# B and C of the SSM and the first MLP columns: weights as the stationary operand, high and low tokens as one moving operand

## The chip, the cores and the metric

The kernel runs on one core of a Trainium2 chip. The metric is the device time of one execution in microseconds (us), as the median of several runs.

## The reference

Two layers on 256 tokens of 2048 features, in float32: multi-head latent attention and an MLP, then a Mamba-2 mixer (SSM) and an MLP. Each part works on an RMS-normed input and adds to the residual. What the change touches:

```python
def ssm_mixer(h, w_in, conv_w, conv_b, ...):
    zxbcdt = h @ w_in                        # 2048 -> z 4096, x 4096, B 1024, C 1024, dt 64
    z, xbc, dt = jnp.split(zxbcdt, ...)
    xbc = jax.nn.silu(causal_depthwise_conv(xbc, conv_w, conv_b))   # width 4, along the tokens
    xs, b_in, c_in = jnp.split(xbc, ...)     # 8 groups: 512 of x, 128 of B, 128 of C each
    ...                                      # scan: C B^T with decay, times x dt; plus D x
    y = y * jax.nn.silu(z)                   # the gate, then an RMS norm for each group
    return (y * norm_g) @ w_out

def squared_relu_mlp(h, w_in, w_out):        # 2048 -> 8192 -> 2048
    u = jax.nn.relu(h @ w_in)
    return (u * u) @ w_out
```

## The kernel before

**Products.** Each float32 operand is split into a high part in a short format (`fp32r`, by a copy on ScalarE, L102 for weights and L299 for activations) and a low part (the rest, by a subtract on VectorE, L103 and L300). A product is three matmuls: high x high, low x high, high x low. Weights come in pieces of 512 KB (128 rows x 1024) through the pool `raw` (`wraw`, or `wrx` in the MLP), are split into `wh` and `wl`, and are converted three pieces ahead of their use. The activations are kept transposed (features on the partitions, `xT`, `us`, `yT`) and are the stationary operand: a matmul loads 128 features x 128 tokens and streams 512 weight columns. The result, 128 tokens x 512 columns, has to be transposed by TensorE before it can be the input of the next product: four 128x128 transposes into one bank (`transposed`, L310), then a split.

**Order.** TensorE's order is written out by hand; the other engines follow the order in which the code issues their work. `later(n, fn)` puts a step off by n ticks; `block` ticks after each key of two pieces. So what `later(0, ...)` names runs after the next key.

**Boundaries.** `finalize` adds a block to the residual, multiplies by the gain and puts the transposes off by a tick; the factor 1/rms (`rs`, from `set_rstd`) is applied later, to the results. `self.xT` lies in eight tiles of pool `xt`, high and low apart, either by feature quarter or (`by_tile`, for the MLPs) by feature half and token tile. The attention uses the same eight tiles for q, k, p and transposed p.

**MLP.** Of eight column pairs (two blocks of 512 hidden columns each) seven are computed by a scheme of seven products of half size (`M1`, `N3` to `N7`, `M2`), on combinations of quarters of the input that `combinations` builds in three steps (`one`, `two`, `three`). The first pair is computed plainly: tokens ("c", 0, j, o), o = 0 to 7, one piece each. `plan` writes the order of all pieces and `mlp_body` walks through it, with a clock (`move`) that puts transposes and steps at their times.

**SSM.** `SSM_ORDER` lists the blocks: B0, d0, C0, x0, B1, x1, C1, and so on. B and C are computed 512 columns (four groups) at a time, `bc_block`; ScalarE applies `rs`, TensorE transposes, and `conv` works with the tokens along the free axis (L1083 to L1095). `cb_group` makes the product of B and C for a group. `narrow_block` (L344) computes dt with the weights stationary and 256 tokens moving. `z_block` computes the gate; `gate` multiplies on GpSimd, takes square sums and a root, scales (L1317) and sends the transposes of the gated y a step later. The o blocks multiply these with `w_out`.

Of the kernel before, what the change touches and what calls it, by code (L numbers as in the profile page):

```python
# [42 lines left out]
C_INV, C_DTB, C_ALOG, C_CW, C_CB, C_END = 848, 880, 944, 1008, 1200, 1248  # L43
# [171 lines left out]
class Trunk:  # L215
    def __init__(self, tc, ctx, d, out):
# [6 lines left out]
        self.xtp = pool("xt", 8)  # L223
# [112 lines left out]
    def narrow_block(self, key, tiles, then, lag=1):  # L336
# [5 lines left out]
        for kt in range(16):  # L342
            for i in range(2):
                nc.tensor.matmul(acc[:, :256], w[kt // 8][:, kt % 8], tiles[kt // 4][i][:, kt % 4],  # L344
                                 start=kt == 0 and i == 0, stop=kt == 15 and i == 1)
# [13 lines left out]
    def from_tiles(self, tiles, off=0):  # L359
        def lhs(kt, t):  # L360
            h, lo = tiles[(kt + off) // 4]
# [5 lines left out]
    def boundary_begin(self, gain, by_tile=False):  # L367

        self.nx = {} if by_tile else [None] * 4
        self.by_tile = by_tile  # L370
        self.nx_ssq = self.stat(8)
        self.nx_gain = gain
# [6 lines left out]
    def finalize(self, nb, accs, wide=True):  # L379
        nc = self.nc  # L380
        g = self.gain_tile(self.nx_gain[nb])
        if not self.by_tile:
            self.nx[nb] = (self.ktile(self.xtp), self.ktile(self.xtp))
        elif nb % 2 == 0:
            for t in range(2):
                self.nx[nb // 2, t] = [self.ktile(self.xtp).rearrange("p a b -> p (a b)").rearrange("p (k n) -> p k n", n=P)
                                       for _ in range(2)]
        for t in range(2):
            if self.by_tile:
                h, lo = (v[:, 4 * (nb % 2):4 * (nb % 2) + 4] for v in self.nx[nb // 2, t])  # L390
            else:
                h, lo = (v[:, :, t * P:(t + 1) * P] for v in self.nx[nb])
# [12 lines left out]
    def set_rstd(self, ssq):  # L405
# [6 lines left out]
        self.nc.gpsimd.tensor_scalar(keep[:, 2:4], r, 0.5, None, ALU.mult)  # L412
        self.rs = [keep[:, t:t + 1] for t in range(2)]
        self.rsh = [keep[:, 2 + t:3 + t] for t in range(2)]

    def add_residual(self, nb, accs):
        for t in range(2):
            x = self.x[t][nb]
            self.nc.vector.tensor_tensor(x, accs[t], x, ALU.add)


    def start(self, seq):
# [28 lines left out]
        self.rs_pool = [self.c.tile([P, 4], F32, name=f"rs{i}") for i in range(2)]  # L451
        self.phase = 0
        self.xT = [(self.ktile(self.xtp), self.ktile(self.xtp)) for _ in range(4)]

        def split_x(j, ks):
            h, lo = self.xT[j]
# [41 lines left out]
    def combinations(self, mp, xa):  # L498
# [4 lines left out]

        def whole(i, t):
            pool = "rx" if len(f) < 3 else "ry"
            f[i, t] = self.flow.pools[pool].tile([P, 1024], F32, tag=pool, name=self.name("xf"))
            h, lo = (v.rearrange("p k n -> p (k n)").bitcast(F32) for v in xa[i, t])
            nc.vector.tensor_tensor(f[i, t], h, lo, ALU.add)
            return f[i, t]

        def put(name, src, pool):
            S[name] = [(self.ktile(self.xtp).rearrange("p a b -> p (a b)") if pool is None else
                        pool.tile([P, 1024], F32R, name=self.name("s" + name))).rearrange("p (k n) -> p k n", n=P)
                       for _ in range(2)]
            self.split_out(*[v.rearrange("p k n -> p (k n)") for v in S[name]], src)
# [5 lines left out]
        def one():  # L521
# [3 lines left out]
            put("N5", a22, mp)  # L525
            f["s1"] = a22

        def two():
            put("N7", less(f[0, 1], f[0, 1], f[0, 0]), mp)
            put("N6", less(f[0, 0], f[0, 0], f["s1"]), mp)  # L530
# [3 lines left out]
        def three():  # L534
            put("N3", f[1, 0], None)
# [3 lines left out]
    def mlp_body(self, mp, layer, gain):  # L539
# [12 lines left out]
        def relu(src, t):  # L552
            r = self.scratch()
            nc.scalar.activation(r, src, AF.Relu, scale=rs[t])
            return r

        def lhs_x(kt, t):
            return [v[:, kt % 8] for v in xa[kt // 8, t]]
# [5 lines left out]
        S["M1"], S["N4"], S["M2"] = xa[0, 0], xa[1, 1], xa[1, 0]  # L564
# [69 lines left out]
        for tok in tokens:  # L634
            key = (tok[0], layer) + tok[1:]
            if tok[0] == "s":
# [8 lines left out]
                products([bank[name]], key, lambda k, t: [x[:, k] for x in S[name]], d,  # L645
# [4 lines left out]
            elif tok[0] == "c":  # L650
                _, p, j, o = tok
                if o == 0:
                    out["c"] = pair_of_banks(self.yp if j else self.acc)
                products(out["c"], key, lhs_x, o, o == 0, o == 7)
                if o == 7:
                    for t in range(2):
                        turn(relu(out["c"][t], t), p, j, t, TR[4])
                    if j:
                        when(3, steps[2])
                if o % 2:  # L660
                    self.tick()
                move(2.72)
            else:
# [4 lines left out]
                if o == 3:  # L668
                    self.add_residual(nb, out.pop(nb))
# [134 lines left out]
    def mla_body(self, mp, gain):  # L804
# [90 lines left out]
        def s1(u, name):  # L895
# [3 lines left out]
            dst = self.ktile(self.xtp, F32)  # L899
# [22 lines left out]
        def s2(u):  # L922
            qT, kT = U[u]["qT"], U[u]["kT"]
            p = self.ktile(self.xtp, F32).rearrange("p a b -> p (a b)")
# [25 lines left out]
        def s3(u):  # L950
            p = U[u]["p"]
            pT = self.ktile(self.xtp, F32).rearrange("p a b -> p (a b)")
# [58 lines left out]
        self.boundary_begin(gain, True)  # L1011
# [26 lines left out]
    def ssm_body(self, sp, dp, gain):  # L1038
# [11 lines left out]
        fm = {}  # L1050
        xg = [None] * GROUPS
        early = [True]
# [23 lines left out]
        def conv(ev, ct, dst, lag):  # L1076

            def half(j):
                b = self.bank(early[0])
                for k in range(2):  # L1080
                    for t in range(2):
                        o = k * 256 + t * P
                        nc.tensor.transpose(b[:, o:o + P], ev[t][:, (2 * j + k) * P:(2 * j + k + 1) * P], self.ident)  # L1083
                a = self.scratch()
                for k in range(2):
                    c = ct + 2 * j + k
                    wc = lambda i: cst[:, C_CW + 4 * c + i:C_CW + 4 * c + i + 1]
                    s, o = b[:, k * 256:(k + 1) * 256], a[:, k * 256:(k + 1) * 256]
                    nc.scalar.activation(o, s, AF.Identity, bias=cst[:, C_CB + c:C_CB + c + 1], scale=wc(3))
                    for i in (2, 1, 0):  # L1090
                        m = 3 - i
                        nc.vector.scalar_tensor_tensor(o[:, m:256], s[:, 0:256 - m], wc(i), o[:, m:256], ALU.mult, ALU.add)
                th = self.scratch()
                nc.scalar.activation(th, a, AF.Tanh, scale=0.5)
                nc.vector.scalar_tensor_tensor(dst(j), th, 1.0, a, ALU.add, ALU.mult)  # L1095
            self.later(lag, lambda: half(0))
            self.later(lag + 1, lambda: half(1))

        def evac(accs):
            ev = []  # L1100
            for t in range(2):
                e = self.scratch()
                nc.scalar.activation(e, accs[t], AF.Copy, scale=rs[t])
                ev.append(e)
            return ev

        def bc_block(name, i):
            accs = self.block([("si", name, i, q) for q in range(4)], xT)
            t = self.ktile(self.k4, F32)
            fm[name, i] = t  # L1110
            conv(evac(accs), (32 if name == "B" else 40) + 4 * i,
                 lambda j: t[:, 2 * j:2 * j + 2].rearrange("p a b -> p (a b)"), 0)
# [50 lines left out]
        def cb_group(g):  # L1163
            B, C = fm["B", g // 4][:, g % 4], fm["C", g // 4][:, g % 4]
            b = self.bank(early[0])
            nc.tensor.matmul(b[:, 0:256], B[:, 0:P], C, start=True, stop=True)
            nc.tensor.matmul(b[:, 256:384], B[:, P:256], C[:, P:256], start=True, stop=True)
            t = sp.tile([P, 384], F32, tag="cb", name=f"cb{g}", bufs=5)
# [10 lines left out]
        def x_block(g):  # L1179
# [59 lines left out]
            if g >= 4:  # L1239
                self.later(0, lambda: cb_group(g))  # L1240
# [52 lines left out]
        def z_block(g):  # L1293
# [11 lines left out]
            def gate():  # L1305
# [10 lines left out]
                for t in range(2):  # L1316
                    nc.vector.scalar_tensor_tensor(ws[t], xg[g][t], r[:, t:t + 1], ng, ALU.mult, ALU.mult)  # L1317
                    self.later(0, lambda t=t: self.transposes(ws[t], yT[g][0], yT[g][1], t, False))
                self.later(0, lambda: gated.add(g))
# [6 lines left out]

        for step in SSM_ORDER:
            kind, i = step[0], int(step[1])
            if step == "C1":
                early[0] = False  # L1330
            if kind in "BC":
                bc_block(kind, i)
                if step == "C0":
                    for g in range(4):
                        self.later(2 + g % 2 + 4 * (g // 2), lambda g=g: cb_group(g))
                    self.pump = pump
# [9 lines left out]
            else:  # L1346
                self.boundary_begin(gain, True)
# [12 lines left out]
SSM_ORDER = ["B0", "d0", "C0", "x0", "B1", "x1", "C1", "x2", "z0", "x3", "z1", "x4", "z2", "o0", "x5", "z3", "x6", "z4", "o1",  # L1360
             "x7", "z5", "z6", "o2a", "z7", "o2b", "o3"]
# [7 lines left out]
PAUSE = 2.7  # L1369

# [57 lines left out]
def sequence(d):  # L1428
# [23 lines left out]
    def mlp(i):  # L1452
        mi, mo = d[f"mi{i}"], d[f"mo{i}"]
        unit = [seven(i, p, mi) for p in range(8)]
        for tok in plan():
            if tok[0] == "s":
                seq.append(lambda flow, t=tok: [unit[t[1]](flow, *t[2:])])
            else:
                kind, p, j, o = tok
                src = mi[o // 2, 2 * p + j] if kind == "c" else mo[2 * p + o // 2, j]  # L1460
# [6 lines left out]
    col = lambda name, i: {"z": 0, "x": 8, "B": 16, "C": 18}[name] + i  # L1467
    si = lambda name, i: [add(("si", name, i, q), d["si"][q, col(name, i)]) for q in range(4)]
    so = lambda k, nb: add(("so", k, nb), d["so"][k, nb])
    for step in SSM_ORDER:  # L1470
        kind, i = step[0], int(step[1])
        if kind in "xzBC":
            si(kind, i)
        elif kind == "d":
# [30 lines left out]

def narrow(w):
# [57 lines left out]
```

## Time and profile before

| | us |
|---|---|
| median of 3 runs | 2300.64 (2300.29 to 2302.55) |
| the profiled execution | 2299.97 |
| its span, first to last instruction | 2298.2 |
| TensorE busy in it (PE) | 2285.3 |
| VectorE busy (DVE) | 1908.4 |
| ScalarE busy (ACT) | 1392.4 |
| GpSimd busy (POOL) | 213.2 |

The granted TensorE clock was 1.000 over the span. In the rows L12 is line 12 of the kernel, `out<-in` are tile names, `xN` is a count of instructions. A timeline row gives start, duration, engine and, in brackets, idle time before it and what ended it. The rows of the grouped lines give busy time, mean ns of one, and idle time before them. PEld is TensorE's loading of the stationary operand, which has a record of its own. Matmuls overlap their neighbours in the records, so the distance between starts says more than a duration.

### The profile page before, as it was taken

The page shows a single profiled execution, that of the slowest core. Times are in us where ns is not written, and L with a number is a line of the kernel's source. Part 1 is how long each engine was busy: PE and PEld are TensorE (multiplying, and loading weights), DVE is VectorE, ACT ScalarE, POOL GpSimd, SP SyncE. Part 2 cuts the span into 40 slices and gives each one's busy share as a digit, 9 for nine tenths or more (in the row PEclk, how much of TensorE's full clock was granted, in tenths as well). Part 3 has the DMA queues.
Part 4 walks back from the last instruction along what each step waited for, and adds up shares of the span by engine and source line. Part 5 has one row for each costly group of instructions (what it writes and reads, how often), then busy time and mean ns, then how long its engine had stood idle before and what let it go on. Part 6 is the DMA issues. An engine that isn't in the chain of part 4 may idle for free.

```text
span 2298.2 us, 30453 instructions
## 1 busy us (share of the span) xinstructions
PE 2285.3 (99%) x10929; PEld 1897.3 (83%) x10929; DVE 1908.4 (83%) x2318; ACT 1392.4 (61%) x1947; POOL 213.2 (9%) x229
## 2 busy tenths in 40 slices
PE   9999999999999999999999999999999999999999
PEld 7898888888888888888888878878888888888887
DVE  7786697999899897687889678667989989989885
ACT  7775476566566656564656545544666666666663
POOL 1430000000000000000122112110000000000000
PEclk9999999999999999999999999999999999999999
DMA  8435687887887878667877777766688788888874
GB/s 316 149 126 158 198 233 244 262 239 251 264 244 245 267 209 274 203 211 245 282 258 255 248 272 239 229 187 204 206 256 236 247 265 248 243 270 239 254 224 163
DMA packets 161912, 538.07 MB, mean 234 GB/s; under 512 B 17680, under 2 KB 26832, under 8 KB 160736
## 3 DMA queue, kind: packets, MB, share of 16 engines
q1 hardware_dynamic: 151264, 502.44, 66.1%
q0 software_dynamic: 8096, 29.41, 7.9%
q10 hardware_dynamic: 2400, 4.27, 0.5%
q8 instruction: 86, 1.41, 0.2%
q14 instruction: 66, 0.54, 0.1%
HBM read 529.65 MB, written 6.41 MB: 233 GB/s over the span
## 4 chain that ended last, share of the span: by engine, by line
PE 94%; DVE 3%; DMA 1%; issue 1%; POOL 1%; ACT 1%; SPq 0%; DVEq 0%; ACTq 0%; POOLq 0%
PE acc L325 12%; PE acc L326 12%; PE acc L329 12%; PE yp L595 9%; PE yp L596 9%; PE yp L594 9%; PE st L595 7%; PE st L596 7%; PE st L594 7%; PE sm L310 2%; DVE wl L103 1%; DMA wraw<-mi 1%; PE acc L594 1%; PE acc L596 1%; PE acc L595 1%
## 5 line engine op out<-in xcount | busy, mean ns | idle before, releaser
L102 ACT ACTIVATE wh<-wraw 128x1024 fp32r<-128x1024 f32 (+1 forms) x818 | 857.9, 1053 | 606.4 <-PE acc L326 290.8
L103 DVE TENSOR_TENSOR wl<-wraw,wh 128x1024 fp32r<-128x1024 f32 (+1 forms) x818 | 984.5, 1218 | 239.0 <-ACT wh L102 228.0
L594 PE MATMUL yp<-wh,k 128*128 128x512 f32 x896 | 349.8, 390 | 0.0
L595 PE MATMUL yp<-wl,k 128*128 128x512 f32 x896 | 348.9, 389 | 0.5 <-DVE wl L103 0.5
L596 PE MATMUL yp<-wh,k 128*128 128x512 f32 x896 | 348.9, 389 | 0.0
L325 PE MATMUL acc<-wh,xt 128*128 128x512 f32 x704 | 279.3, 397 | 0.8 <-ACT wh L102 0.8
L326 PE MATMUL acc<-wh,xt 128*128 128x512 f32 x704 | 274.4, 390 | 0.0
L102 ACT ACTIVATE wh<-wrx 128x1024 fp32r<-128x1024 f32 x168 | 177.9, 1059 | 136.9 <-PE yp L596 105.0
L103 DVE TENSOR_TENSOR wl<-wrx,wh 128x1024 fp32r<-128x1024 f32 x168 | 203.8, 1219 | 37.3 <-ACT wh L102 37.2
L595 PEld LDWEIGHTS yp<-wl,k 128*128 128x128 f32 x896 | 168.3, 188 | 36.0 <-DVE wl L103 1.4
L596 PEld LDWEIGHTS yp<-wh,k 128*128 128x128 f32 x896 | 168.2, 188 | 34.9
L594 PEld LDWEIGHTS yp<-wh,k 128*128 128x128 f32 x896 | 168.2, 188 | 34.7
L325 PE MATMUL acc<-wh,k 128*128 128x512 f32 x496 | 196.2, 396 | 0.0
L326 PE MATMUL acc<-wh,k 128*128 128x512 f32 x496 | 193.2, 389 | 0.0
L329 PE MATMUL acc<-wl,xt 128*128 128x512 f32 x704 | 188.3, 389 | 0.0
L594 PE MATMUL st<-wh,xt 128*128 128x512 f32 x448 | 176.8, 395 | 0.0
L595 PE MATMUL st<-wl,xt 128*128 128x512 f32 x448 | 174.8, 390 | 0.0
L596 PE MATMUL st<-wh,xt 128*128 128x512 f32 x448 | 174.8, 390 | 0.0
L325 PEld LDWEIGHTS acc<-wh,xt 128*128 128x128 f32 x704 | 132.2, 188 | 30.8 <-ACT wh L102 3.2
L326 PEld LDWEIGHTS acc<-wh,xt 128*128 128x128 f32 x704 | 132.3, 188 | 27.6 <-issue 1.2
L329 PEld LDWEIGHTS acc<-wl,xt 128*128 128x128 f32 x704 | 132.1, 188 | 27.7
L199 POOL DMA_DIRECT2D wrx<-mi x56 | 49.1, 876 | 1140.8 <-DVE wl L103 1034.9
(307 smaller groups left out, 3449.5 us busy)
## 6 DMA issues: line engine op xcount, KB each, us to landing
wraw<-mi SPq DMA_DIRECT2D x256, 512.0 KB, 5.2
wraw<-mo SPq DMA_DIRECT2D x256, 512.0 KB, 5.3
wraw<-si SPq DMA_DIRECT2D x160, 512.0 KB, 5.0
wraw<-so SPq DMA_DIRECT2D x64, 512.0 KB, 4.8
wrx<-mi SPq DMA_DIRECT2D x56, 512.0 KB, 5.1
wrx<-mi POOLq DMA_DIRECT2D x56, 512.0 KB, 8.0
wraw<-wo SPq DMA_DIRECT2D x32, 512.0 KB, 3.9
taps<-xD SPq DMA_DIRECT2D x16, 768.0 KB, 8.4
```

Of the source, the lines that this page charges most:

```text
L102: self.last = nc.scalar.activation(h[:, v], raw[:, v], AF.Copy)
L103: self.last_lo = nc.vector.tensor_tensor(lo[:, v], raw[:, v], h[:, v].bitcast(F32), ALU.subtract)
L199: nc.gpsimd.dma_start(st["b11"].tile, quarter(d, 1, 0), accum_op=ALU.add)
L310: self.nc.tensor.transpose(b[:, j * P:(j + 1) * P], src[:, j * P:(j + 1) * P], self.ident)
L325: nc.tensor.matmul(accs[t][:, :n], ah, wh[:, q, :], start=first and kt + q == 0, stop=False)
L326: nc.tensor.matmul(accs[t][:, :n], al, wh[:, q, :], start=False, stop=False)
L329: nc.tensor.matmul(accs[t][:, :n], lhs(kt + q, t)[0], wl[:, q, :], start=False, stop=en and q == nk - 1)
L594: nc.tensor.matmul(b, ah, wh, start=first and q == 0, stop=False)
L595: nc.tensor.matmul(b, ah, wl, start=False, stop=False)
L596: nc.tensor.matmul(b, al, wh, start=False, stop=last and q == 1)
```

## The change

1. **Weights stationary** for B, C and the first column pair of each MLP. `column_unit` takes a weight piece of 1024 rows x 128 columns as eight stationary operands: the high weights multiply high and low tokens as one moving operand of 2 x 256 columns, the low weights the 256 high tokens. The two halves of the bank are added afterwards. The result has the columns on the partitions, so nothing is transposed. For this, high and low of `xT` lie in one tile (`pair`), by feature quarter throughout; `xt` has four such tiles, the attention shares them (q with k, p with transposed p), and N3 is written over the quarter of the input that is free by then.
2. **B, C group by group**: `SSM_ORDER` has a step b for each group (four pieces) between the x and z blocks. `rs` is applied by a product with `row`, the factors of the tokens along the free axis on all partitions, which two small matmuls make. In the MLP the factor is applied squared when the first pair's products are added to the residual.
3. **Gated y a step later**: its transposes stand two ticks behind the gate, not one.

```diff
+    def pair(self, dt=F32R):
+        return self.xtp.tile([P, 2, 4, 256], dt, tag="xt", name=self.name("xt"))
...
-    def add_residual(self, nb, accs):
+    def add_residual(self, nb, accs, scale=None):
...
+            if scale:
+                self.nc.vector.scalar_tensor_tensor(x, accs[t], scale[t], x, ALU.mult, ALU.add)
...
+    def column_unit(self, acc, unit, xw, half):
+        h, lo = (v.rearrange("p (k n) -> p k n", n=P) for v in unit)
+        nc = self.nc
+        high = lambda k: nc.tensor.matmul(acc.rearrange("p (i n) -> p i n", i=2), h[:, k], xw[2 * half + k // 4][:, :, k % 4],
+                                          start=half == 0 and k == 0, stop=half == 1 and k == 7)
+        low = lambda k: nc.tensor.matmul(acc[:, 0:256], lo[:, k], xw[2 * half + k // 4][:, 0, k % 4], start=False, stop=False)
+        for k in range(8):
+            for fn in ((low, high) if half and k == 7 else (high, low)):
+                fn(k)
...
         def three():
-            put("N3", f[1, 0], None)
+            for c in range(2):
+                src = f[1, 0][:, c * 512:(c + 1) * 512].rearrange("p (k n) -> p k n", n=P)
+                self.split_out(part(0, 1, c, 0), part(0, 1, c, 1), src)
+            S["N3"] = operand(0, 1)
...
+        def column(p, j, f, acc):
+            if f == 0:
+                us[p, j] = (self.ktile(self.k4), self.ktile(self.k4))
+            h, lo = us[p, j]
+            r = self.scratch()[:, 0:256]
+            nc.scalar.activation(r, acc[:, 256:512], AF.Copy)
+            nc.vector.tensor_tensor(r, acc[:, 0:256], r, ALU.add)
+            nc.scalar.activation(r, r, AF.Relu)
+            nc.scalar.activation(r, r, AF.Square)
+            self.split_out(h[:, f], lo[:, f], r)
...
-                if o % 2:
+                if o % 2 == 0:
                     self.tick()
-                move(2.72)
+                move(2.78)
...
+        def rs_row():
+            c = self.scratch()[:, :S]
+            for t in range(2):
+                nc.vector.tensor_scalar(c[:, t * P:(t + 1) * P], tri[:, P:256], rs[t], None, ALU.mult)
+            b = self.bank(False)
+            for t in range(2):
+                nc.tensor.matmul(b[:, t * P:(t + 1) * P], c[:, t * P:(t + 1) * P], self.ident, start=True, stop=True)
+            nc.vector.tensor_copy(row, b[:, :S])
+        self.later(1, rs_row)
+
+        def bc_columns(g):
+            accs = [self.acc_tile() for _ in range(2)]
+            for half in range(2):
+                for i in range(2):
+                    self.column_unit(accs[i], self.flow.next(("sb", i, g, half))[1], self.xT, half)
+                    if i == 0:
+                        self.tick()
+            s, a, th = (self.scratch() for _ in range(3))
+            of = lambda v: v.rearrange("p (i n) -> p i n", i=2)
+            for i in range(2):
+                nc.scalar.activation(of(s)[:, i], accs[i][:, 256:512], AF.Copy)
+                nc.vector.tensor_tensor(of(s)[:, i], accs[i][:, 0:256], of(s)[:, i], ALU.add)
+            def conv():
+                nc.vector.tensor_tensor(of(s), of(s), row.unsqueeze(1).to_broadcast([P, 2, S]), ALU.mult)
...
+            self.later(0, conv)
+            self.later(2, lambda: cb_group(g))
...
-                    self.later(0, lambda t=t: self.transposes(ws[t], yT[g][0], yT[g][1], t, False))
-                self.later(0, lambda: gated.add(g))
+                    self.later(1, lambda t=t: self.transposes(ws[t], yT[g][0], yT[g][1], t, False))
+                self.later(1, lambda: gated.add(g))
...
-SSM_ORDER = ["B0", "d0", "C0", "x0", "B1", "x1", "C1", "x2", "z0", "x3", "z1", "x4", "z2", "o0", "x5", "z3", "x6", "z4", "o1",
-             "x7", "z5", "z6", "o2a", "z7", "o2b", "o3"]
+SSM_ORDER = ["b0", "d0", "x0", "b1", "x1", "b2", "x2", "z0", "b3", "x3", "z1", "b4", "x4", "z2", "o0", "b5", "x5", "z3",
+             "b6", "x6", "z4", "o1", "b7", "x7", "z5", "z6", "o2a", "z7", "o2b", "o3"]
...
+def column_of(o):
+    return 2 * (o // 4) + o % 2, o % 4 // 2
```

More of the change, by code (lines that the diff above doesn't have):

```diff
@@ L651, in mlp_body @@
                 _, p, j, o = tok
[L652 to L659, printed above, removed]
-                if o % 2:
+                f, half = column_of(o)
+                if half == 0:
+                    pool = self.yp if j else self.acc
+                    out["c", f] = pool.tile([P, 512], F32, tag=pool.name, name=self.name("cf"))
+                self.column_unit(out["c", f], self.flow.next(key)[1], xa, half)
+                if half:
+                    column(p, j, f, out.pop(("c", f)))
+                if o == 7 and j:
+                    when(3, steps[2])
+                if o % 2 == 0:
                     self.tick()
-                move(2.72)
+                move(2.78)
             else:
@@ L668, in mlp_body @@
                 if o == 3:
-                    self.add_residual(nb, out.pop(nb))
+                    self.add_residual(nb, out.pop(nb), None if p else self.rssq)
                 move(2.72)
@@ L1099, in evac @@
[L1099 to L1112, printed above, removed]
+        row = sp.tile([P, S], F32, name="rsrow")
@@ L1325, in o_block @@
             return self.block([("so", 2 * i + q, nb) for q in range(2)], self.from_tiles(yT[2 * i:2 * i + 2]))
+        self.pump = pump
         for step in SSM_ORDER:
             kind, i = step[0], int(step[1])
[L1329 to L1336, printed above, removed]
+            if kind == "b":
+                bc_columns(i)
             elif kind == "d":
@@ L1471, in sequence @@
         kind, i = step[0], int(step[1])
-        if kind in "xzBC":
+        if kind in "xz":
             si(kind, i)
+        elif kind == "b":
+            for half in range(2):
+                for j in range(2):
+                    seq.append(part(("sb", j, i, half), d["sbc"][j, i, half]))
         elif kind == "d":
```

143 lines of the change are left out of this document (67 added, 76 removed).

## The prediction

> **What bounds the kernel now.** I read the page first: its shares of busy time and the chain that ended last.
>
> ```profile
> PE 2285.3 (99%) x10929; PEld 1897.3 (83%) x10929; DVE 1908.4 (83%) x2318; ACT 1392.4 (61%) x1947; POOL 213.2 (9%) x229
> ...
> PE 94%; DVE 3%; DMA 1%; issue 1%; POOL 1%; ACT 1%; SPq 0%; DVEq 0%; ACTq 0%; POOLq 0%
> ```
>
> The kernel is TensorE's own instruction stream: 94% of the chain and 99% busy. What the change is worth is therefore (a) what it takes out of and puts into that stream, and (b) which of the few waits of TensorE it ends or makes. VectorE at 83% is the next candidate. Since busy matmuls overlap in the records, I price a matmul by the distance from one start to the next. The timeline of TensorE and the chain in order of time give it.
>
> ```profile
> 962.82 0.39 PE L325 MATMUL acc<-wh,xt 128*128 128x512 f32 x1
> ...
> 965.54 0.39 PE L325 MATMUL acc<-wh,xt 128*128 128x512 f32 x1
> ...
> 977.53 0.60 PE L1083 MATMUL sm<-cst,s 128*128 128x128 f32 x4
> 977.89 0.48 PE L325 MATMUL acc<-wh,xt 128*128 128x512 f32 x1
> 978.20 0.39 PE L326 MATMUL acc<-wh,xt 128*128 128x512 f32 x1
> ```
> ```profile
> 973.86 3.83 PE sm L344 x32
> ...
> 2283.76 11.20 PE acc L703 x72
> ```
>
> From 962.82 to 965.54 lie the 12 matmuls of one weight piece: 2.72 us, 227 ns each for 512 columns. The 32 matmuls of `narrow_block` have 256 columns and a weight load each: 3.83 / 32 = 120 ns. The last block (24 of 512 columns, 48 of 256, by its code) confirms both: 24 x 0.227 + 48 x 0.120 = 11.2 us. A group of four transposes moves the second matmul behind it from 977.53 + 0.227 = 977.76 to 978.20, so it costs 0.44 us.
>
> **The change on TensorE.** Of old, a 128x128 block of weights costs three times 128 columns of output for each of two token tiles: 768 columns. In `column_unit` it is 512 (high weights on high and low tokens) and 256 (low weights on high tokens): 768 again. Only the number of instructions grows. B and C were 4 blocks of 16 x 6 = 384 matmuls; the first column pairs of the two MLPs are another 384, as these rows show (each has two partners of 64, on L595 and L596).
>
> ```profile
> L594 PE MATMUL acc<-wh,xt 128*128 128x512 f32 x64 | 25.2, 393 | 0.0
> L594 PE MATMUL yp<-wh,xt 128*128 128x512 f32 x64 | 25.1, 392 | 0.0
> ...
> L1083 PE MATMUL sm<-cst,s 128*128 128x128 f32 x20 | 3.0, 272 | 0.0
> ...
> L1083 PE MATMUL yp<-cst,s 128*128 128x128 f32 x12 | 1.8, 273 | 0.0
> ```
>
> So 768 matmuls become 512 of 512 columns and 512 of 256 columns: 512 x 0.120 - 256 x 0.227 = 61.4 - 58.1 = **+3.3 us**. Bounds: if the short ones cost half of a long one, 0; with 0.130 in the alternation of long and short, +8.5. I take the row, since there too every matmul follows its own load.
>
> The Trainium skill (page "TensorE: Matmul & The Clock Gate", section "Back-to-back issue gap") gives 262 and 518 cycles at 2.4 GHz for 256 and 512 columns, 109 and 216 ns, by which this term would be about +0.7 us, an estimate. The measured distances, 120 and 227 ns, are both 11 ns longer, so the trace decides.
>
> Transposes that go: all 32 of B and C (L1083, 8 groups), and in each MLP two column blocks x two token tiles = 4 groups, 8 in all. 16 x 0.44 = **-7.0 us**. `rs_row` adds two 128-column products, half a group: **+0.25 us**. The products of `cb_group` stay. The scaling by rs[t] of B and C becomes a product with `row`, that of the MLP columns goes into `add_residual` as rs squared, at one VectorE instruction either way.
>
> **The gated y.** Where does TensorE wait at all? The waits view has one long entry for it, and the timeline one example:
>
> ```profile
> PE sm L310 <- DVE s L1317: 5.5, 5, 1.6
> ```
> ```profile
> 1204.42 2.21 POOL L283 TENSOR_TENSOR st<-st,mhalf 128x2 f32<-128x2 f32 x1 [9.36 <-DVE st L282]
> ```
> ```profile
> 1209.21 1.75 DVE L1317 SCALAR_TENSOR_TENSOR s<-xtm,st,gb 128x512 f32<-128x512 f32 x1
> ```
> ```profile
> 1211.11 0.63 PE L310 MATMUL sm<-cst,s 128*128 128x128 f32 x4 [1.65 <-DVE s L1317]
> ```
>
> The transposes of the gated y stand one step (two pieces, 5.4 us) behind the gate in TensorE's order, and the gate's chain (product on GpSimd, square sums, root, two scalings on VectorE) ends up to 1.6 us after their turn. One step later they have 5.4 us more, over three times the longest wait. **-5.5 us**. What is late next? The o blocks that read y come at least four pieces (10.9 us) behind the moved transposes, except o2a, whose first two pieces (5.4 us) read the earlier group; I cost it at 0. The two scratch tiles of the gate stay occupied 5.4 us longer, and the B, C chain wants three of the same seven: that wait would be one of VectorE, ScalarE or GpSimd, and is part of the next term.
>
> **VectorE and ScalarE.** Here the change costs work, and I ask where there is room.
>
> ```profile
> 284.00:295.00 11.00, 11.00 (x50) 9.13 (x49) 11.00 (x11) 7.24 (x7) 0.00 (x0) 1.00 0.72 227
> 295.00:306.00 11.00, 11.00 (x53) 8.91 (x53) 10.97 (x11) 7.64 (x10) 0.00 (x0) 1.00 0.64 213
> 306.00:317.00 11.00, 11.00 (x51) 9.09 (x50) 10.94 (x11) 6.82 (x7) 1.08 (x1) 1.00 0.82 239
> 317.00:328.00 11.00, 11.00 (x50) 9.13 (x49) 10.19 (x10) 6.50 (x7) 0.87 (x1) 1.00 0.86 259
> ```
> ```profile
> 294.68 2.35 DVE L103 TENSOR_TENSOR wl<-wraw,wh 128x1024 fp32r<-128x1024 f32 x2
> ...
> 295.73 0.39 PE L594 MATMUL yp<-wh,xt 128*128 128x512 f32 x1
> ...
> 295.96 0.49 PE L595 MATMUL yp<-wl,xt 128*128 128x512 f32 x1
> ```
>
> The columns are span, PE, PEld, DVE and ACT busy time. In the first 45 us of an MLP VectorE is full (third number), because the combinations of `one` and `two` stand there, and the piece at 295.73 gets its low half at the very moment at which TensorE wants it. Into this stretch and the next go, for each MLP, 8 columns with an add and a subtract of 256 elements, in place of 4 subtracts of 512, and four sums cut in two.
>
> ```profile
> 977.73 0.42 DVE L347 COPY s<-sm 128x256 f32<-128x256 f32 x1 [2.42 <-PE sm L344]
> ```
> ```profile
> 274.24 1.28 DVE L396 TENSOR_TENSOR s<-x,gb 128x512 f32<-128x512 f32 x2
> ```
> ```profile
> 273.07 0.39 PE L594 MATMUL acc<-wh,xt 128*128 128x512 f32 x1
> ...
> 278.51 0.60 PE L310 MATMUL yp<-cst,s 128*128 128x128 f32 x4
> ```
>
> A 256 instruction takes 0.42 us; two of 512 take 1.28, so in a row each counts 0.60, some 0.08 less than alone, and one of 256 about 0.34. 16 x 0.34 - 4 x 0.60 + 4 x 0.07 = +3.3 us for each MLP. Against it: the tick now comes after the first piece of the c block, so that the last transposes of the boundary, at 278.51 after the two pieces that begin at 273.07, come one piece earlier, and `one`, which stands behind their halves in VectorE's order, can start 2.7 us sooner. Their input is ready at 274.24 + 1.28 = 275.5, before TensorE gets there at 273.07 + 8 x 0.347 = 275.85. Idle time of 0.9 us in the last two windows is also there. TensorE itself comes 4 x 0.44 - 16 x 0.05 = 0.9 us sooner. 3.3 - 2.7 - 0.9 + 0.9 = 0.6 us short for each MLP. On top, the subtract of a column needs three passes of ScalarE (Relu, Square, Copy) after the add; if VectorE stands still for them, that is up to 3 x 0.41 us a column:
>
> ```profile
> L1263 ACT ACTIVATE mt<-mt 128x256 f32<-128x256 f32 x64 | 26.1, 407 | 0.5
> ```
>
> Bounds for each MLP: 0 (the order fills the pause with other work and the head start carries) to 0.6 + 8 x 1.2 = 10 us. I take 1.0, near the lower end, because in the first two windows VectorE, whose order holds many such subtracts behind a ScalarE copy (every low half is one), is idle 0.03 us in 22. Both MLPs: **+2 us**.
>
> In the SSM, B and C bring 2 x 0.42 + 0.68 = 1.5 us of VectorE for each group (two adds, the product with `row`), and the convolution now falls between the x and z blocks. VectorE has room there (1075 to 1560 us, grouped lines: 75.8 us of idle time before the low halves alone):
>
> ```profile
> L103 DVE TENSOR_TENSOR wl<-wraw,wh 128x1024 fp32r<-128x1024 f32 x164 | 202.3, 1246 | 75.8 <-ACT wh L102 75.1 <-DMA cm<-cumD 0.4
> ```
>
> `cb_group` follows its B, C pieces by three ticks (16 us) for a chain of some 7 us of work. I take **+1 us** (0 to 6) for places where the new step meets the tail of x.
>
> Loads keep their size and queue (512 KB by SP). The pairs in `xt` are freed as late as the later of the old two, and the attention uses four of them in the rhythm in which it used eight halves: 0. If the write of N3 into half of a tile makes the M1 products of the other half wait, that is up to 2 us in each MLP; it belongs to the upper end.
>
> **Sum.** Profiled execution 2299.97 us (span 2298.2 and 1.8 around it): -7.0 + 3.3 + 0.25 - 5.5 + 2 + 1 = -5.95, so 2294.0. The median lies 0.67 above that execution: **2294.7 us**.
>
> **The rivals.** *No change:* VectorE and ScalarE give back most of the 9 us: each column halts VectorE for half of the three passes, 16 x 0.6 = 9.6 us, instead of the 2 taken: 2302. For it: VectorE at 11.00 of 11.00. Against it: three pieces of lead elsewhere, and pauses only in the first 45 us.
>
> *Slower:* the subtract waits in VectorE's queue for the whole ScalarE chain, with the low halves of the next pieces behind it and TensorE behind those. 20 us in both MLPs in place of 2: 2312.7. It decides as soon as the new waits pass 13.5 us (2291.7 without any, 2305.2 the bound), 0.84 us a column.
>
> *Slower, by the weights:* a load is not covered behind a matmul of 256 columns. The loads are long enough:
>
> ```profile
> L344 PEld LDWEIGHTS sm<-xt,wh x32: 188/192/192, 28.6 to 975.4; 128*128 128x128 f32 x32
> ```
>
> 256 more instructions x 0.19 us would be 49 us: 2344. Against it stand the 120 ns of that very line, less than one load. The Trainium skill (same page, "What overlaps and what doesn't") has loads overlap running matmuls only in other row groups, which speaks for this rival; the 120 ns of full-height loads disagree.
>
> That the change does not do what it says has little room: TensorE's order is written out by hand, and the transposes are no longer in it.
>
> **How the numbers follow.** About 0.2%, 4.6 us, is what a measurement of this kernel can tell from no change. Forecast 0.58 (2290 to 2296, all faster), no change 0.24 (2296 to 2305), the wait on ScalarE or its like 0.15, uncovered loads 0.03. The range starts at 2290 (no new waits, and short matmuls a little cheaper) and ends at 2304, which leaves the two slower cases out.
>
> **What would show it.** Right: 64 transposes less; low column products at starts 120 ns apart from the next, 347 for a pair; no wait of the y transposes for L1317's successor; VectorE busy some 18 us more (2 x 3.3 and 8 x 1.5). Wrong: TensorE idle for the low halves in the first 70 us of an MLP (VectorE rival), or pairs well above 350 ns (weights).

## The result and the profile after

The changed kernel takes 2307.6 us (2304.97 to 2310.83 in eight runs) against 2300.9 us of the kernel before in as many runs: a ratio of 1.0026, 95% interval 1.0016 to 1.0037. It is slower by some 6 us (6.7 by the medians) where 2294.7 was forecast: about 13 us more than forecast. The profiled execution after took 2310.83 us, the longest of the eight, so its own times stand some 3 us above the median.

First the page of the changed kernel: busy time by engine, and the shares of the chain that ended last.

```profile
PE 2290.7 (99%) x11125; PEld 1908.9 (83%) x11125; DVE 1930.3 (84%) x2379; ACT 1398.8 (61%) x1997; POOL 208.5 (9%) x233
...
PE 84%; DVE 9%; DMA 3%; issue 2%; POOL 1%; ACT 1%; SPq 0%; DVEq 0%; ACTq 0%; POOLq 0%
```

Busy shares look as before (99%, 83 to 84%). The chain doesn't: TensorE falls from 94% to 84% of it and VectorE rises from 3% to 9%. More of the end is now handed on by VectorE, and that sends the reader to the waits of TensorE, here those of the changed kernel (total, count, longest, in us).

```profile
PE sm L1199 <- DVE k L303: 5.1, 2, 2.8
PE acc L332 <- DVE wl L103: 2.6, 4, 1.3
PE st L620 <- DVE wl L103: 1.7, 2, 0.9
PE sm L1199 <- DVE bc L1142: 1.6, 1, 1.6
...
PE cf L427 <- DVE wl L103: 1.1, 1, 1.1
```

The wait of the y transposes for the gate, 5.5 us before, is gone. In its place the product of B and C in `cb_group` (L1199) waits 6.7 us, and 5.1 of them not for B and C but for L303, the low half of a transposed block.

Where in the kernel is the time? The first matmuls of the two MLPs, in the timelines of before (the first stands in the prediction, at 273.07) and after, divide it.

```profile
951.04 0.39 PE L325 MATMUL acc<-wh,xt 128*128 128x512 f32 x1
...
1618.82 0.47 PE L594 MATMUL acc<-wh,xt 128*128 128x512 f32 x1
```
```profile
272.70 0.39 PE L425 MATMUL cf<-xt,wh 128*128 128x512 f32 x1
...
952.17 0.39 PE L425 MATMUL acc<-xt,wh 128*128 128x512 f32 x1
...
1628.34 0.48 PE L425 MATMUL cf<-xt,wh 128*128 128x512 f32 x1
```

From the first MLP's first matmul to the SSM's: 677.97 us before, 679.47 after, +1.5. SSM: 667.78 and 676.17, +8.4. The second MLP to the end of the span: 679.4 and 680.7, +1.3. So nearly all lies in the SSM, for which the forecast's terms give -6.1 (8 groups of transposes -3.5, half of the short matmuls +1.65, `rs_row` +0.25, gated y -5.5, VectorE +1): 14.5 us off in this execution. The timeline after shows one of the long waits.

```profile
1178.75 1.03 PE L313 MATMUL sm<-cst,s 128*128 128x128 f32 x8
...
1181.95 2.45 DVE L1139 SCALAR_TENSOR_TENSOR s<-s,cst,s 128x255 f32<-128x255 f32 x6
...
1185.45 0.69 DVE L1142 SCALAR_TENSOR_TENSOR bc<-s,s 128x512 f32<-128x512 f32 x1
...
1187.26 1.28 DVE L303 TENSOR_TENSOR k<-sm,k 128x512 fp32r<-128x512 f32 x2
...
1188.00 1.22 PE L1199 MATMUL sm<-bc 128*128 128x256 f32 x2 [2.76 <-DVE k L303]
```

At 1178.75 the eight transposes of a gated y fill two banks called `sm`; the pool has no more. Their split (L303) stands in VectorE's order behind the convolution of B and C (L1139, L1142) and a step of x (L1251), and comes 8.5 us later. B and C themselves are ready at 1186.14; the first of the two banks is free only when the first of the two splits ends, at about 1187.9, and TensorE stands idle for 2.76 us. The granted clock falls during the other long wait (2.35 us, to 1120.61) and at the end of this one, as these rows show (span, then busy time of PE, PEld, DVE, ACT, POOL, then the granted clock, DMA share, GB/s):

```profile
1119.70:1126.40 6.70, 5.80 (x70) 5.18 (x71) 5.24 (x11) 3.37 (x11) 1.80 (x2) 0.50 0.49 143
1188.00:1191.30 3.30, 3.30 (x9) 2.73 (x10) 3.30 (x6) 0.00 (x0) 0.25 (x1) 0.50 0.48 176
```

TensorE works at a granted clock of 0.50 for 5.8 us behind the one wait and for 3.3 us behind the other: half of that, 4.6 us, is lost on top of the 6.7. The mean clock of this execution was 0.998; six of the other seven had 0.999 and one 1.000, so the median run lost less.

### The profile page after: what moved, and what is told of

Its sections match the earlier page's. It is cut to its first block, busy times and chain, and to the rows that moved or that the text cites. A ratio compares the mean times of both kernels' runs of the same rounds, so it can differ in the third digit from the quotient of the medians.

```text
span 2309.0 us, 30976 instructions
## 1 busy us (share of the span) xinstructions
PE 2290.7 (99%) x11125; PEld 1908.9 (83%) x11125; DVE 1930.3 (84%) x2379; ACT 1398.8 (61%) x1997; POOL 208.5 (9%) x233
## 4 chain that ended last, share of the span: by engine, by line
PE 84%; DVE 9%; DMA 3%; issue 2%; POOL 1%; ACT 1%; SPq 0%; DVEq 0%; ACTq 0%; POOLq 0%
PE acc L328 10%; PE acc L329 10%; PE acc L332 10%; PE yp L620 8%; PE yp L621 8%; PE yp L619 8%; PE st L620 7%; PE st L621 7%; PE st L619 7%; DVE wl L103 4%; PE sm L313 2%; PE acc L425 1%; DMA wraw<-mi 1%; DVE xtm L1243 1%; DVE wraw L183 1%
## 5 line engine op out<-in xcount | busy, mean ns | idle before, releaser
L620 PE MATMUL yp<-wl,k 128*128 128x512 f32 x896 | 349.0, 389 | 0.2 <-DVE wl L103 0.2
L328 PE MATMUL acc<-wh,xt 128*128 128x512 f32 x576 | 229.2, 398 | 0.4 <-ACT wh L102 0.4
L329 PE MATMUL acc<-wh,xt 128*128 128x512 f32 x576 | 225.2, 391 | 0.0
L620 PEld LDWEIGHTS yp<-wl,k 128*128 128x128 f32 x896 | 168.2, 188 | 35.4 <-DVE wl L103 0.9
L620 PE MATMUL st<-wl,xt 128*128 128x512 f32 x448 | 174.8, 390 | 0.0
L332 PE MATMUL acc<-wl,xt 128*128 128x512 f32 x576 | 154.3, 390 | 1.9 <-DVE wl L103 1.9
L332 PE MATMUL acc<-wl,k 128*128 128x512 f32 x496 | 132.9, 390 | 0.7 <-DVE wl L103 0.7
L620 PE MATMUL st<-wl,sN 128*128 128x512 f32 x336 | 131.1, 390 | 1.7 <-DVE wl L103 1.7
L619 PE MATMUL st<-wh,sN 128*128 128x512 f32 x336 | 132.1, 393 | 0.0
```

What stands on the lines that cost most here:

```text
L328: nc.tensor.matmul(accs[t][:, :n], ah, wh[:, q, :], start=first and kt + q == 0, stop=False)
L329: nc.tensor.matmul(accs[t][:, :n], al, wh[:, q, :], start=False, stop=False)
L332: nc.tensor.matmul(accs[t][:, :n], lhs(kt + q, t)[0], wl[:, q, :], start=False, stop=en and q == nk - 1)
L619: nc.tensor.matmul(b, ah, wh, start=first and q == 0, stop=False)
L620: nc.tensor.matmul(b, ah, wl, start=False, stop=False)
```

## The experiments

Ratios are to the kernel before in the runs of the same chip, with 95% intervals. The changed kernel stands at 1.0026. The kernel before had medians of 2299.5 to 2300.9 us in these batches, so a measured time is held against an expected one through the ratio.

Two theories at first. **A:** the loss is a meeting: the y transposes, a step later, hold both `sm` banks when `cb_group` comes to its turn. **B:** the loss lies in the new B, C step itself (its VectorE work, the price of its matmuls), and the later y still brings its 5.5 us.

**e1: the later y alone, in the kernel before.**

```diff
-  self.later(0, lambda t=t: self.transposes(ws[t], yT[g][0], yT[g][1], t, False))
-self.later(0, lambda: gated.add(g))
+  self.later(1, lambda t=t: self.transposes(ws[t], yT[g][0], yT[g][1], t, False))
+self.later(1, lambda: gated.add(g))
```

> The kernel before with part 3 alone: the transposes of the gated y two ticks behind the gate. Theory A (the loss of the whole change comes from B, C and the moved transposes meeting in TensorE's order, part 3 alone does what the prediction said): the five waits of the y transposes go, 5.5 us, nothing takes their place: 2295.4 us against 2300.9. Theory B (the scaling steps of the gate are only a symptom of a full VectorE, the wait comes back elsewhere): 2299 to 2301.

0.9985 (0.9977 to 0.9994), some 3.4 us faster. That is less than A's 5.5 us and more than the 1.9 that B left at most. The gate's waits are gone, but A's "nothing takes their place" did not hold; from its timeline:

```profile
1214.11 1.03 PE L310 MATMUL sm<-cst,s 128*128 128x128 f32 x8
...
1222.14 1.28 DVE L300 TENSOR_TENSOR k<-sm,k 128x512 fp32r<-128x512 f32 x2
...
1222.87 0.70 PE L1166 MATMUL sm<-k,k 128*128 128x256 f32 x2 [2.27 <-DVE k L300]
```

The same meeting, once, in the old kernel: L1166 is `cb_group`'s product there. It is the move of y that makes it, with or without the new B and C.

**e2: the y transposes back to their old place, in the changed kernel** (the same lines, 1 to 0).

> The changed kernel without part 3: y transposes one tick behind the gate again. Theory A: the products of B and C no longer wait for the two small banks that the y transposes hold (5.1 us of idle time and some 2 us of slower clock behind them), but the gate's own waits may return (0 to 5 us): 2301 to 2306 against 2307.6. Theory B: the banks play no part, the gate's waits return in full: 2311 to 2313.

1.0052 (1.004 to 1.0065): slower than the change by some 6 us. From its waits:

```profile
PE sm L313 <- DVE s L1348: 9.7, 10, 2.0
PE sm L1199 <- DVE bc L1142: 3.2, 3, 2.5
```

The wait for the bank is gone as A said, so the banks do play a part, against B. But the wait for the gate comes back at 9.7 us in ten places, where the kernel before had 5.5 in five, and A had allowed at most 5. A's number missed; B's number, 2311 to 2313, held, though not for B's reason. What it says of part 3: moving y pays, in the changed kernel more than in the old; its meeting with `cb_group` takes it back.

**e3: `cb_group` one tick later**, so that the banks are free by then.

```diff
-            self.later(2, lambda: cb_group(g))
+            self.later(3, lambda: cb_group(g))
```

> The changed kernel with the product of B and C one tick (two pieces, 5.4 us) later. Theory A: all three waits of that product go (6.7 us idle and some 2 to 3 us of slower clock behind them): 2298 to 2300 against 2307.6. Theory B: VectorE is behind anyway, and the wait moves to the low halves of the weights: 2305 to 2307.

0.9994 (0.9985 to 1.0003), 7.4 us less than the change, as A expected. No wait of L1199 is left, and the mean clock is 1.000. From its waits:

```profile
PE acc L332 <- DVE wl L103: 3.5, 6, 1.3
```

So the waits for the bank, the one for B and C, and the clock behind them are over half of the 13 us missed. Whether it was the bank or B, C that came too late, e3 does not tell, since a tick helps both.

**e9: the product of B and C in a bank of another pool**, at its old time. The far part is copied out at once, because it would hold one of the blocks' banks.

```diff
-            b = self.bank(False)
+            b = self.bank("acc")
...
-            def far_part():
-                with behind("last"):
-                    nc.scalar.activation(t[:, P:256], b[:, P:256], AF.Copy, scale=0.125)
-
-            self.later(0, far_part)
+            with behind("last"):
+                nc.scalar.activation(t[:, P:256], b[:, P:256], AF.Copy, scale=0.125)
```

> The changed kernel, with the product of B and C in a bank of the big pool (acc) in place of one of the two small banks, and all of it copied out in one step. Bank theory (two of the three waits are for a small bank that the y transposes hold until VectorE has split them): 2.5 and about 2 of the 2.9 us go, the third wait (1.8 us, for the convolved B and C themselves) stays: 2302 to 2304 against 2307.6. Rival (the convolution is late in all three): the waits keep their size, now named after the convolution's last step: 2307.

1.0003 (0.9994 to 1.0012), some 5.3 us less than the change, where the bank theory gave 3.6 to 5.6 and its rival next to nothing. The timeline at the place shown above:

```profile
1171.98 1.03 PE L313 MATMUL sm<-cst,s 128*128 128x128 f32 x8
...
1178.69 0.69 DVE L1142 SCALAR_TENSOR_TENSOR bc<-s,s 128x512 f32<-128x512 f32 x1
...
1179.52 0.67 PE L1199 MATMUL acc<-bc 128*128 128x256 f32 x2 [1.06 <-DVE bc L1142]
...
1180.49 1.29 DVE L303 TENSOR_TENSOR k<-sm,k 128x512 fp32r<-128x512 f32 x2
```

Now the product runs before the split that it used to wait for, and what is left of the wait is for B and C, 1.06 us here and 2.7 in two places in all, against 6.7 in three before. The mean clock is 1.000 again. The bank carries most of it; B and C are late as well, but less.

**e8: the meeting taken out of e1**: y later, and `cb_group` a tick later for the groups from 4 on, all else as before.

```diff
-                self.later(0, lambda: cb_group(g))
+                self.later(1, lambda: cb_group(g))
```

> The kernel before with the y transposes a tick later (e1_gate_only, 2296.2 us) and, for groups 4 to 7, the product of B and C a tick later too. If that product waits because the y transposes hold the two small banks until VectorE has split them (2.3 us, once, in e1_gate_only), the wait goes: 2293 to 2295. If VectorE is simply behind there, the wait moves: 2296.

**0.9971** (0.9959 to 0.9982), 2294.15 us against 2300.85: faster than both kernels, and as the bank theory expected. From its timeline, where e1 had the wait:

```profile
1214.04 1.03 PE L310 MATMUL sm<-cst,s 128*128 128x128 f32 x8
...
1222.09 1.27 DVE L300 TENSOR_TENSOR k<-sm,k 128x512 fp32r<-128x512 f32 x2
...
1226.67 0.59 PE L1166 MATMUL sm<-k,k 128*128 128x256 f32 x2
```

That is 6.7 us from three numbers in three calls of `later`: two move y (e1's edit), one moves `cb_group`.

**e6: the MLP part alone**, with the SSM wholly as before and y at its old time. The edit is long; its core:

```diff
-SSM_ORDER = ["b0", "d0", "x0", "b1", ...
+SSM_ORDER = ["B0", "d0", "C0", "x0", ...
...
-    a["sbc"] = columns(wi[:, 8192:10240]).reshape(2, 8, 2, P, 1024)
+    a["si"] = pieces(wi[:, :10240])
```

> The MLP part alone: first column pairs with the weights stationary, the SSM wholly as before (blocks of four groups, y transposes one tick behind the gate). Theory C: 2.5 to 4 us more than before, 2302 to 2304. Rival D: 0 to 2 us less than before.

1.0012 (1.0004 to 1.0021), +2.8 us (0.9 to 4.8), as C expected. By the forecast's terms this part was +0.15 (8 groups -3.5, short matmuls +1.65, VectorE +2).

**e5: e3 with the old first column pairs of the MLPs**, on the new layout of the tokens.

```diff
-                self.column_unit(out["c", f], self.flow.next(key)[1], xa, half)
-                if half:
-                    column(p, j, f, out.pop(("c", f)))
+                products(out["c"], key, lhs_x, o, o == 0, o == 7)
+                if o == 7:
+                    for t in range(2):
+                        turn(relu(out["c"][t], t), p, j, t, TR[4])
```

> The kernel with the product of B and C one tick later (e3_cb_later, 2299.2 us), and in both MLPs the first column pair computed as before (three matmuls, transposes, rs applied to the result); the SSM stays changed. Theory C (the MLP part costs: its short and long pairs are 352 and not 347 ns, and VectorE's low halves come late at two places for each MLP): 2.5 to 4 us less, 2295 to 2297. Rival D (the MLP part is worth its 3.5 us of transposes and what is left of the loss lies in the SSM): 2300 to 2302.

1.001 (1.0001 to 1.0019): some 3.7 us more than e3, far from C's 2.5 to 4 less and above D's range, which its interval still reaches. It brought waits of its own:

```profile
PE acc L616 <- DVE wl L103: 3.2, 2, 1.6
```

These stand 22 us into each MLP, where the kernel before has none, so this is not the old MLP, and the run doesn't settle between C and D.

**e4: high and low of a token pair next to each other**, so that the 512 moving elements lie in one stretch. It asks whether the moving operand's layout sets the price of a pair.

```diff
+    def near_pair(self):
+        return self.xtp.tile([P, 4, 2, 256], F32R, tag="xt", name=self.name("xt")).rearrange("p k i n -> p i k n")
```

> The changed kernel with high and low tokens of a feature row side by side (512 elements in a run) in place of two runs of 256 that lie 1024 elements apart. If the two runs are why a matmul of 512 columns takes 235 ns to the next start here and 227 elsewhere: pairs of 347 ns and 2.6 us less over 512 pairs, 2305. If the 8 ns come from the following short matmul's load: pairs stay at 352 ns, 2307.6.

1.0025 (1.0014 to 1.0035), as the change. The interval alone could hide 2.6 us, but the trace does not: from a long matmul to the next short one it is 235 ns in the median, as in the changed kernel. The layout isn't it.

**e7: e3 with eight high matmuls and then eight low ones** instead of turn about.

```diff
+        for k in range(7 if half else 8):
+            high(k)
         for k in range(8):
-            for fn in ((low, high) if half and k == 7 else (high, low)):
-                fn(k)
+            low(k)
+        if half:
+            high(7)
```

> e3_cb_later with the order inside a weight piece changed: first the eight long matmuls with the high weights, then the eight short ones with the low weights. If a pair takes 352 ns because long and short alternate: 347 ns, 2.6 us less over 512 pairs. If each costs that by itself, 352 ns stay. Besides, the low half of a piece is wanted 1.6 us later, so waits for low halves at column pieces (1.2 us in each run) go: 2295 to 2298 against 2299.2; or 2298 if the pairs stay.

0.9994 (0.9985 to 1.0003), level with e3. The waits for low halves at column pieces are gone as expected, but those of the MLPs' other products (L623, L620 in e3) grew from 1.9 to 2.6 us. The timelines of the changed kernel, at two places, and of e7 give the price of a pair:

```profile
1089.65 0.39 PE L425 MATMUL acc<-xt,wh 128*128 128x512 f32 x1
...
1091.38 0.39 PE L425 MATMUL acc<-xt,wh 128*128 128x512 f32 x1
...
1095.89 0.40 PE L425 MATMUL acc<-xt,wh 128*128 128x512 f32 x1
...
1097.66 0.40 PE L425 MATMUL acc<-xt,wh 128*128 128x512 f32 x1
```
```profile
1088.14 2.00 PE L425 MATMUL acc<-xt,wh 128*128 128x512 f32 x8
1089.98 1.12 PE L427 MATMUL acc<-xt,wl 128*128 128x256 f32 x8
1090.93 1.78 PE L425 MATMUL acc<-xt,wh 128*128 128x512 f32 x7
```

Turn about, five pairs take 1.73 us at one place and 1.77 at the other: 346 and 354 ns each. Grouped, a piece of eight pairs takes 2.79 us, 349. Taken over whole pieces, the median pair is 352 ns in the changed kernel and 348 in e7, so at 512 pairs the order is worth some 2 us by the records, no more than these runs resolve.

What e3 and e7 still wait for in the SSM are low halves of weights (L332: 3.5 and 3.6 us). The convolution of B and C stands in VectorE's order among the products of x with the filter there. e10 and e11, two ways out of e7, test whether that makes the low halves late.

**e10: the convolution two ticks later** and `cb_group` two more behind it; the two scratch tiles of the convolution are taken only then.

```diff
-            s, a, th = (self.scratch() for _ in range(3))
+            s = self.scratch()
...
             def conv():
+                a, th = self.scratch(), self.scratch()
...
-            self.later(0, conv)
-            self.later(3, lambda: cb_group(g))
+            self.later(2, conv)
+            self.later(5, lambda: cb_group(g))
```

> e7_high_first (2299.2 us) with the convolution two ticks later and the product of B and C two ticks after that, behind the tail of the x block before. If the low halves in the SSM come late (3.6 us in six waits) because convolution and tail of x meet on VectorE: 2295 to 2297. If VectorE is late there for another reason (its products of x slowed by GpSimd, which works at the same time): 2298 to 2300.

0.998 (0.9971 to 0.9989), about 3.2 us less than e7, as expected if the two meet, and the waits for low halves shrink to:

```profile
PE acc L332 <- DVE wl L103: 1.1, 3, 0.4
```

**e11: the ticks of the steps b1 to b7 a piece later.** It was meant to keep the filter's products on VectorE apart from GpSimd's gate product, beside which they run slower. The changed kernel's timeline shows both cases:

```profile
1091.10 4.07 POOL L1342 TENSOR_TENSOR xtm<-s,xtm 128x512 f32<-128x512 f32 x2 [6.21 <-DVE s L1332]
1091.54 2.47 DVE L1238 TENSOR_TENSOR taps<-taps,cw 128x1536 f32<-128x1536 f32 x1
1093.94 1.78 DVE L1239 TENSOR_TENSOR xtm<-xtm,cw 128x512 f32<-128x512 f32 x1
1095.65 1.75 DVE L1238 TENSOR_TENSOR taps<-taps,cw 128x1536 f32<-128x1536 f32 x1
1097.32 0.68 DVE L1239 TENSOR_TENSOR xtm<-xtm,cw 128x512 f32<-128x512 f32 x1
```

```diff
-                    if i == 0:
+                    if i == (g > 0):
                         self.tick()
```

> e7_high_first with the ticks of steps b1 to b7 after the second piece of a pair, not the first, so that the products of x with the filter are issued a piece (2.8 us) later against the gate's product on GpSimd. If the two slow each other (VectorE's filter products took 54.3 us in e3_cb_later and 44.3 before, the difference all in SSM steps where both run): 48 us or less, fewer waits for low halves, 2295 to 2297. If the overlap is not what makes the low halves late: 2299.

0.9997 (0.9989 to 1.0006): no gain. The filter's products (L1238 and L1239) still take 52.0 us, against 54.3 in e3 and 44.3 before, so the edit hardly did what it was for. Whether the overlap with GpSimd costs the kernel time stays open; e10 lost its waits with the overlap as it was (54.2 us).

**e12: e10 and e11 together.**

> Both of e10_conv_later and e11_tick. If the two causes add up: 2293 to 2295, level with e8_gate_cb (2294.2), which has neither B, C nor MLP columns; this is the best that the change can give with TensorE's pairs at 348 ns. If they are one cause: as the better of the two.

0.9981 (0.9972 to 0.999), 2294.66 us against 2299.51, as e10: e11's later tick adds nothing. The changed kernel, mended in its order alone, gains some 4.4 us, where 6 were forecast for it. That its time equals the forecast 2294.7 is luck, since the kernel before was faster in this batch. It comes no further than e8 (0.9971), which has none of its new products.

## Why the prediction was wrong

**The step that failed** is in "The gated y", the answer to "What is late next?", and its echo in the VectorE term. The prediction went through who reads the moved y transposes (the o blocks, at least 10.9 us behind) and who shares their scratch tiles, and costed the rest at nothing. It did not ask who else uses the two banks that the transposes write, and how long they hold them. For `cb_group` it priced the chain of B and C (three ticks for 7 us of work: +1 us, 0 to 6), and not the bank that its own product needs. And 7 us of work is not the time until it is done: from the last matmul on a group's columns to its convolved B and C lie 9.5 to 19 us in the trace after, 18 to 19 in the three groups that wait. The bank comes back only when VectorE has done the split, and VectorE's order has the convolution before it. In the profiled execution that was two waits of 5.1 us in all, one of 1.6 for B and C, and 4.6 us of clock behind the long ones; e1, e3, e8 and e9 show it from four sides, and e3 puts it at 7.4 us in the median.

**The second miss** is the same VectorE term: the low halves of x weights beside the convolution (2.6 us here, 3.5 in e3). "VectorE has room there" was read from idle time over 485 us. It is not there in the places where the convolution meets the filter. e10 puts it at 3.2 us. Together 10.6 of some 13 us.

**Right, with sizes.** Transposes: 64 gone. The rows of the grouped lines after count 400, against 396 + 36 + 32 before:

```profile
L313 PE MATMUL sm<-cst,s 128*128 128x128 f32 x364 | 52.4, 272 | 0.0
...
L313 PE MATMUL yp<-cst,s 128*128 128x128 f32 x36 | 5.4, 272 | 0.0
```

Short matmuls: 352 ns for a pair and not 347 makes +3.3 into 3.3 + 512 x 0.005 = +5.9, inside the bound of 8.5. Gated y: -5.5 was about right for the move without its meeting. Alone it gave 3.4 us with the meeting (e1), 6.7 with `cb_group` out of the way (e8). VectorE in the MLPs: the waits stand in the first 70 us as named, one of 1.1 us and two below 1.0 (L427, L620), but e6 puts the whole MLP part at +2.8 where the terms gave +0.15; of the 2.6 between them 1.3 is the pairs (256 x 5 ns), and the rest is within e6's interval. VectorE's busy time rose by 21.9 us, forecast 18, but that is luck: 9.9 us of it are the filter's products of x (44.3 us before, 54.2 after), which take longer beside GpSimd and were not in the forecast.

**The parts.** The forecast's terms without waits give parts 1 and 2 together -7.0 + 3.3 + 0.25 + 3 = -0.5 and part 3 the rest. Within the intervals that division held: e12 with all three parts (0.9981) and e8 with part 3 and `cb_group` moved (0.9971) are level, each with its meeting taken out. Of the rivals, "no change" had VectorE giving back the gain in the MLPs, and "slower" had a subtract waiting for ScalarE there; both named the wrong place. The loss had the slower rival's form, a step in VectorE's order that others stand behind, but in the SSM and by way of a bank. Loads were covered: of 437 pairs in the trace after, 426 took 340 to 361 ns, against the 539 that an uncovered load would add up to (347 + 192).

The shares are differences of medians from different batches, each with an interval of some 2 us either way; some 2 us of the 13 have no experiment of their own.

## What to carry over

When a step is moved, go through every buffer that it holds, and not only its input and its readers: who takes the next one of the same pool, and what stands in the freeing engine's order before the instruction that gives it back. Room on an engine is read in the windows where the new work lands; an average over the stage says nothing of them. And try each part alone: here a change of order in three lines (e8) was worth at least as much as the whole mended change (e12).

## What the runs showed of the hardware

In the changed kernel the granted clock fell to 0.50 behind waits of 2.35 and 2.76 us. Behind e1's wait of 2.27 us it stayed at 1.00. In e4, which waits at the same two places, it fell behind 2.33 us and stayed at 1.00 behind 2.75. These are the windows of e1, then those behind the two waits of e4:

```profile
1220.00:1223.00 3.00, 0.73 (x4) 0.30 (x3) 3.00 (x5) 2.36 (x3) 0.67 (x1) 1.00 0.93 356
1223.00:1226.00 3.00, 3.00 (x15) 2.53 (x16) 3.00 (x10) 0.00 (x0) 0.00 (x0) 1.00 0.79 239
```
```profile
1118.00:1121.00 3.00, 3.00 (x40) 2.66 (x41) 3.00 (x5) 1.19 (x4) 0.00 (x0) 0.51 0.47 168
1184.00:1187.00 3.00, 2.96 (x14) 2.53 (x15) 3.00 (x5) 0.16 (x1) 0.29 (x1) 1.00 0.54 215
```

So nearly the same gap cost the clock in one execution and not in another; its length alone does not decide.

The Trainium skill (page "TensorE: Matmul & The Clock Gate", section "What's actually happening") gives half rate after at least one idle window of about 3.4 us. All five gaps were shorter, and three of them cost the clock; what decides, these cases don't tell.

On VectorE a product of 1536 elements took 2.47 us beside GpSimd's product and 1.75 without, one of 512 elements 1.78 and 0.68. Over the whole trace after, the products of 1536 elements that lay wholly beside GpSimd's work took 2.46 to 2.85 us, those free of it 1.74 to 1.75. The Trainium skill (page "GPSIMD Engine Reference", section "Specifications") has GpSimd share its SBUF interfaces with VectorE, with contention where an instruction of VectorE has two SBUF inputs; the trace agrees.
